# Stick-breaking attention with queries on partitions: sigmoids and a running product in place of softplus sums

## The chip, the cores and the metric

The kernel runs on one core of one Trainium2 chip. The metric is the device time of one execution in microseconds (us); lower is better.

## The reference, cut to what matters

One step of an encoder over 512 prompt rows (a new stream) and 32 sample rows (a running stream with 1024 cached keys). Layer 0 is a Mamba-2 layer, layer 1 a stick-breaking attention layer with 16 query heads of 64 on 4 key/value heads; each layer has two SwiGLU feed-forward parts (1024 to 2816), a gated embedding part and RMSNorms. All is float32. The part that the change touches:

```python
def sb_block(q, k, v, q0):
    # A[t,s] = sigmoid(z_ts) * prod_{s<j<t} (1 - sigmoid(z_tj)), keys s < t only
    z = jnp.einsum('bqhgd,bkhd->bhgqk', q, k) * (SB_HEAD_DIM ** -0.5)
    mask = jnp.arange(lk)[None, :] < q_pos[:, None]
    log_1m_beta = jnp.where(mask, jax.nn.log_sigmoid(-z), 0.0)
    log_a = z + lax.cumsum(log_1m_beta, axis=4, reverse=True)
    a = jnp.exp(jnp.where(mask, log_a, -jnp.inf))
    return jnp.einsum('bhgqk,bkhd->bqhgd', a, v)

q = h @ w_q;  o = sb_attention(q, k_all, v_all, q_start);  x = x + o @ w_o
```

The weight of a key is a sigmoid times the product of (1 - sigmoid) over all later keys; the reference forms it as exp(z - sum of softplus over this key and the later ones).

## The kernel before

Features lie on partitions and the 544 rows of both groups on columns. A dense product is split: weights and activations go into a high and a low float32 half (`whi`, `wlo`, `xh`, `xl`), and three products of 272 columns make one float32 product. Every instruction is recorded by one helper, so all of them have its line, L193, in the profile; groups are told apart by the names of what they write and read.

`attention(...)` is one stage near the end: query products (8 units of 1024x128 weights, each in two halves of 24 products), attention, output product (two units of 192 products of 272 columns each, one for each `a`). A key/value head is named by a pair (`a`, `b`) with both from 0 to 1; `e` (0 to 3) is the query head within it, `qb` a block of 128 queries, `kb` a block of 128 keys. `kT` holds the keys and `qT` the queries with features on partitions; `kk`, `kl` and `qq` are their halves, with high and low part of a head stacked on the 128 partitions, so that two products give one block of logits. Attention results are written back into `qT`, and `outputs` makes the halves `oh` and `ol` for the output product from it.

Keys lie on partitions. `block(kb, b)` makes the logits of one key block for all four heads of (`a`, `b`), 512 columns, in a PSUM bank `z`; the diagonal block gets the mask as a third product. `softplus` turns them into `zt` (or `run`) with ACT (Abs, Exp, Ln) and DVE; `halve` splits the result into `sh` and `sl`. The sum over later keys within the block is a product with the triangle `ntri`, that over all later key blocks one with a matrix of -1, `nones`, applied to the running sum `run`; both are added into the same bank `z`, two products each. ACT takes the Exp into `at`, and the value products of one key block (`o<-at,vt`, both `b` side by side) go into a bank `o`:

```python
def within():
    add(ps[:n], ntri[:n, :n], sh[:n])
    add(ps[:n], ntri[:n, :n], sl[:n], stop=True)
yield "T", 2 * t_cost(512) + 0.05, within
```

The sample rows run as one more stream of nine blocks (32 new keys, then eight blocks of 128 cached ones, `kc` and `vc`, each loaded by two transfers).

The order of all this comes from a planner, `Plan`. Each step is a generator that yields what it needs: `"get"` and `"put"` of a slot (PSUM banks `z`, `f`, `o`, and buffers), `"wait"` and `"set"` of events, and `("T" | "V" | "S" | "G", cost, emit)` for work on TensorE, VectorE, ScalarE and GpSimd (`"W"` is VectorE too; `either` and `pick` choose the less loaded engine). The planner takes the step that can start first by its costs, by rank where several can, and emits the instructions; the four engines keep that order. `NZ, NF1, NO = 5, 1, 2` gives the eight banks: five for logits, one for query products that are made between attention blocks, two for outputs. The first two units of query products use `z` banks and the later ones `f`. The first output product (`first_mix`) waits for the four blocks of `a` = 0 and the sample; its units then stand between the last blocks of `a` = 1.

Of the kernel before, what the change touches and what calls it, by code (L numbers as in the profile page):

```python
# [28 lines left out]
NZ, NF1, NO = 5, 1, 2  # L29

NSP, NZT, NAT, NRUN = 7, 4, 4, 4

RUNS = 2

BLOCKS = (1, 3, 2, 0), (3, 1, 2, 0)

MERGE, SB = 9, 7
# [3 lines left out]
RMIX, RHEAD = 0.15, 0.3  # L41
# [139 lines left out]
def _body(tc, io):  # L181
# [22 lines left out]
    with ExitStack() as ctx:  # L204
# [1274 lines left out]
        def attention(norm, after, ready, ahead, kT, vtok):  # L1479
            with ExitStack() as keep, \  # L1480
# [5 lines left out]
                def bank(tag, bufs=1):  # L1486
                    return pp.tile([P, 512], F32, tag=tag, name=tag, bufs=bufs)

                def two():
                    return [bank("z", NZ), bank("z", NZ)]  # L1490
# [23 lines left out]
                with tc.tile_pool(name="at", bufs=1, reuse_waits="tile") as tmp:  # L1514
                    ntri = tmp.tile([P, P], F32R, name="ntri")
                    tri = tmp.tile([P, 512], F32, tag="at", name="tri", bufs=NAT)[:, :P]
                    G.affine_select(out=tri, in_=ones, compare_op=ALU.is_ge, fill=0.0, base=0, pattern=[[-1, P]], channel_multiplier=1)
                    V.tensor_scalar(ntri, tri, -1.0, None, op0=ALU.mult)
                    mask = tmp.tile([P, P], BF16, name="mask")
                    G.memset(mask, 0.0)  # L1520
                    G.affine_select(out=mask, in_=mask, compare_op=ALU.is_gt, fill=BIG, base=0, pattern=[[1, P]], channel_multiplier=-1)
                    masks = mask[:TS, :TS].unsqueeze(1).to_broadcast([TS, 16, TS])
                    mask = mask[:, :].unsqueeze(1).to_broadcast([P, 4, P])
                    plan = Plan({"z": NZ, "f": NF1, "o": NO, "raw": 2, "s": NSP, "zt": NZT, "run": NRUN, "at": NAT, "cache": 3, "w": 2}, "a")
# [10 lines left out]
                    def key_parts(a):  # L1535
# [11 lines left out]
                        yield "set", ("keys", a)  # L1547
# [14 lines left out]
                    def softplus(t, z):  # L1562

                        if plan.load("S") <= plan.load("V"):
                            yield "S", s_cost(512, True), lambda: S.activation(t, z, AF.Abs)
                            yield "S", s_cost(512), lambda: S.activation(t, t, AF.Exp, scale=-1.0)
                            yield "S", s_cost(512), lambda: S.activation(t, t, AF.Ln, bias=1.0)
                            yield "W", v_cost(512), lambda: V.scalar_tensor_tensor(out=t, in0=z, scalar=0.0, in1=t, op0=ALU.max, op1=ALU.add)
                        else:
                            yield "W", v_cost(512), lambda: V.tensor_scalar(t, z, 40.0, None, op0=ALU.min)  # L1570
                            yield "S", s_cost(512), lambda: S.activation(t, t, AF.Exp)
                            yield "S", s_cost(512), lambda: S.activation(t, t, AF.Ln, bias=1.0)
                            yield "W", v_cost(512), lambda: V.tensor_tensor(out=t, in0=z, in1=t, op=ALU.max)

                    def halve(t, sh, sl):
                        yield copy(plan, 512, sh, t)
                        yield either(plan, v_cost(512), 1.225, lambda e: e.tensor_tensor(out=sl, in0=t, in1=sh.bitcast(F32), op=ALU.subtract))

                    def parts_tile():
                        return (tmp.tile([P, 512], F32R, tag="sh", name="sh", bufs=NSP),  # L1580
                                tmp.tile([P, 512], F32R, tag="sl", name="sl", bufs=NSP))

                    class Stream:


                        def __init__(self, name, last, halves):
# [297 lines left out]
                    with ExitStack() as keep2:  # L1884
# [10 lines left out]
                        for number, (st, kb) in enumerate(units):  # L1895
                            if st is sample:
                                number -= SB
# [271 lines left out]
```

## Time and profile before

| what | value |
| --- | --- |
| time, three runs | 2328.01, 2328.4, 2331.41 us; median 2328.4 |
| profiled execution | 2331.9 us, of it 2330.2 us span |
| attention stage (first query product to end of output product) | 1656.4 to 1880.2 us |
| DMA | 213 MB, mean 91 GB/s |

The span runs from the first to the last instruction that the profile shows. Busy time is what an engine's instructions are shown to last; matmuls are pipelined, so that one is shown longer than the distance to the next one's start. A row of the groups of instructions reads: engine, operation, output <- inputs, shape, count, then busy time in all and mean ns of one, then idle time just before them and who ended most of it. In a row of the timeline stand the start, the duration, the engine and the operation, and in brackets a wait and its releaser. A row of the windows gives for a stretch its length, then each engine's busy time with its number of instructions, then PEclk, the TensorE clock that was granted as a share of full speed, the DMA share and GB/s.

### The profile page before, as it was taken

How to read it: one execution, taken by the hardware profiler on the slowest of the kernel's cores; microseconds unless marked ns; L12 is line 12 of the kernel's file. 1: busy time of each engine (PE TensorE's matmuls, PEld its weight loads, DVE VectorE, ACT ScalarE, POOL GpSimd, SP SyncE). 2: the span in 40 equal slices, each digit the busy share in tenths (PEclk: the TensorE clock that was granted, in tenths of full speed). 3: DMA queues.
4: the chain of work that ended last, by engine and by line, in shares of the span. 5: the costliest groups of instructions: out<-in, count | busy, mean ns of one | idle time of the engine just before them, and what ended most of it. 6: DMA issues, size and time to landing. Idle time of an engine off the chain costs nothing.

```text
span 2330.2 us, 42548 instructions
## 1 busy us (share of the span) xinstructions
PE 2289.8 (98%) x17763; PEld 2214.1 (95%) x17763; DVE 1700.7 (73%) x2239; ACT 1045.1 (45%) x1531; POOL 584.7 (25%) x563
## 2 busy tenths in 40 slices
PE   9999999999999999999999999999998999999997
PEld 8999999989899999999999999999965799999997
DVE  7777786679677676777857677777688676777857
ACT  5333334557555453333345433333488553333343
POOL 1221222244324122212211122211243222222214
PEclk9999999999999999999999999999999999999999
DMA  5333323333333232233233333332211132333232
GB/s 161 89 91 106 95 73 91 107 97 99 111 92 89 82 117 84 90 109 91 73 101 98 112 100 92 91 109 63 85 49 32 37 118 78 105 97 99 65 104 75
DMA packets 112176, 213.17 MB, mean 91 GB/s; under 512 B 12528, under 2 KB 34672, under 8 KB 111984
## 3 DMA queue, kind: packets, MB, share of 16 engines
q1 hardware_dynamic: 109104, 204.92, 29.7%
q10 hardware_dynamic: 2880, 5.53, 0.7%
q8 instruction: 140, 2.29, 0.4%
q14 instruction: 52, 0.43, 0.1%
HBM read 204.83 MB, written 5.60 MB: 90 GB/s over the span
## 4 chain that ended last, share of the span: by engine, by line
PE 90%; DVE 4%; ACT 3%; issue 1%; POOL 1%; DMA 1%; SPq 0%; DVEq 0%; ACTq 0%; POOLq 0%
PE mm L193 81%; PE z L193 5%; PE aux L193 2%; PE o L193 1%; DVE wlo L193 1%; PE f L193 1%; ACT zt L193 1%; ACT whi L193 1%; POOL ab L193 1%; DVE xl L193 1%; DVE x L193 0%; DMA wraw<-in_wpg 0%; DVE fu L193 0%; ACT L193 0%; DVE rm L193 0%
## 5 line engine op out<-in xcount | busy, mean ns | idle before, releaser
L193 PE MATMUL mm<-xh,whi 128*128 128x272 f32 x2096 | 513.4, 293 | 2.2 <-ACT xh L193 1.2
L193 PE MATMUL mm<-xh,wlo 128*128 128x272 f32 x2096 | 507.1, 290 | 2.2 <-DVE wlo L193 2.2
L193 PE MATMUL mm<-xl,whi 128*128 128x272 f32 x2096 | 508.2, 290 | 0.3 <-DVE xl L193 0.3
L193 PEld LDWEIGHTS mm<-xh,whi 128*128 128x128 f32 x2096 | 359.6, 190 | 10.3 <-issue 7.4
L193 PEld LDWEIGHTS mm<-xh,wlo 128*128 128x128 f32 x2096 | 359.0, 190 | 2.9 <-DVE wlo L193 2.9
L193 PEld LDWEIGHTS mm<-xl,whi 128*128 128x128 f32 x2096 | 358.8, 190 | 0.5 <-DVE xl L193 0.5
L193 ACT ACTIVATE whi<-wraw 128x1024 fp32r<-128x1024 f32 (+3 forms) x217 | 186.6, 861 | 381.1 <-PE mm L193 261.3
L193 PE MATMUL mm<-xfh,whi 128*128 128x272 f32 x1152 | 332.0, 288 | 0.0
L193 PE MATMUL mm<-xfl,whi 128*128 128x272 f32 x1152 | 331.9, 288 | 0.0
L193 PE MATMUL mm<-xfh,wlo 128*128 128x272 f32 x1152 | 331.7, 288 | 0.0
L193 DVE TENSOR_TENSOR wlo<-wraw,whi 128x1024 fp32r<-128x1024 f32 (+3 forms) x252 | 256.1, 1017 | 72.9 <-ACT whi L193 53.6
L193 PE MATMUL mm<-hh,whi 128*128 128x272 f32 x1408 | 291.3, 288 | 0.0
L193 PE MATMUL mm<-hh,wlo 128*128 128x272 f32 x1408 | 290.8, 288 | 0.0
L193 PE MATMUL mm<-hl,whi 128*128 128x272 f32 x1408 | 290.7, 288 | 0.0
L193 ACT ACTIVATE whi<-a 128x1024 fp32r<-128x1024 f32 x127 | 135.0, 1063 | 321.3 <-PE mm L193 211.6
L193 DVE TENSOR_TENSOR wlo<-a,whi 128x1024 fp32r<-128x1024 f32 x145 | 178.4, 1230 | 103.5 <-ACT whi L193 69.0
L193 PEld LDWEIGHTS mm<-hl,whi 128*128 128x128 f32 x1408 | 221.2, 188 | 0.0
L193 PEld LDWEIGHTS mm<-hh,whi 128*128 128x128 f32 x1408 | 221.0, 188 | 0.0
L193 PEld LDWEIGHTS mm<-hh,wlo 128*128 128x128 f32 x1408 | 220.4, 188 | 0.0
L193 PEld LDWEIGHTS mm<-xfh,wlo 128*128 128x128 f32 x1152 | 216.8, 188 | 0.0
L193 PEld LDWEIGHTS mm<-xfl,whi 128*128 128x128 f32 x1152 | 216.7, 188 | 0.0
L193 PEld LDWEIGHTS mm<-xfh,whi 128*128 128x128 f32 x1152 | 216.7, 188 | 0.0
(293 smaller groups left out, 4195.3 us busy)
## 6 DMA issues: line engine op xcount, KB each, us to landing
a<-in_wgu SPq DMA_DIRECT2D x145, 512.0 KB, 4.0
wraw<-in_wd SPq DMA_DIRECT2D x128, 256.0 KB, 2.7
wraw<-in_win SPq DMA_DIRECT2D x41, 512.0 KB, 3.6
wraw<-in_wgu SPq DMA_DIRECT2D x29, 512.0 KB, 3.7
wraw<-in_wd SPq DMA_DIRECT2D x32, 384.0 KB, 3.1
ab<-acs_d SPq DMA_DIRECT2D x16, 512.0 KB, 4.7
wraw<-in_wout SPq DMA_DIRECT2D x16, 512.0 KB, 3.6
wraw<-in_wpg SPq DMA_DIRECT2D x16, 512.0 KB, 3.6
```

The costliest lines, as they stand in the source:

```text
L193: ins = getattr(self.engine, op)(*args, **kw)
```

## The change

Queries lie on partitions now, and keys along the columns. For a piece (`piece`: one `a`, `b`, `qb` and some heads `es`, together up to 512 columns) the logits of each head stand against all its keys, `(qb+1)*128` columns, with the query block as the stationary operand. ACT takes two sigmoids of the bank: `s` = sigmoid(z) into a buffer `p`, and sigmoid(-z) back into the bank. DVE runs a scan along the keys from the last to the first (`scan`), whose result `e` at a key is the product of sigmoid(-z) over it and all later ones; `p` times `e` shifted by one key is the weight. Since values are summed over keys, keys have to be on partitions again: TensorE transposes `p` in blocks of 128x128 into a bank `tr`, and ACT or DVE copies that into `at`. Value products then run per key block for the heads of a group. There are 44 pieces for the prompt.

The sample makes its 32 new keys at once and the 1024 cached ones in two halves of 512 for each (`a`, `b`), 8 pieces; a scan starts from the last result of the later half (`ends`). The cache comes in four loads of keys and four of values. The banks are divided 3 (`z`), 1 (`f`), 2 (`o`), 2 (`tr`). Buffers, ranks and the order of blocks change with it, the first query products use banks of all four kinds (`FIRSTQ`), ScalarE loads the table of sigmoids ahead of the stage in place of that with Exp and Ln, and `ntri`, `softplus`, `halve`, `run` and the products on them are gone.

```diff
-NZ, NF1, NO = 5, 1, 2
-NSP, NZT, NAT, NRUN = 7, 4, 4, 4
-BLOCKS = (1, 3, 2, 0), (3, 1, 2, 0)
+BANKS = {"z": 3, "f": 1, "o": 2, "tr": 2}
+NP, NE, NAT, NSA, NC = 6, 4, 8, 4, 3
+BLOCKS = (2, 3, 1, 0), (3, 2, 1, 0)
+HEADS = ([(0, 1, 2, 3)],), ([(0, 1), (2, 3)],), ([(0,), (1,)], [(2,), (3,)]), ([(0,), (1,)], [(2,), (3,)])
+FIRSTQ = ("z", "z"), ("z", "f"), ("o", "o"), ("tr", "tr")
...
-def softplus(t, z):
-    if plan.load("S") <= plan.load("V"):
-        yield "S", s_cost(512, True), lambda: S.activation(t, z, AF.Abs)
-        yield "S", s_cost(512), lambda: S.activation(t, t, AF.Exp, scale=-1.0)
-        yield "S", s_cost(512), lambda: S.activation(t, t, AF.Ln, bias=1.0)
-        yield "W", v_cost(512), lambda: V.scalar_tensor_tensor(out=t, in0=z, scalar=0.0, in1=t, op0=ALU.max, op1=ALU.add)
...
-def halve(t, sh, sl):
-    yield copy(plan, 512, sh, t)
-    yield either(plan, v_cost(512), 1.225, lambda e: e.tensor_tensor(out=sl, in0=t, in1=sh.bitcast(F32), op=ALU.subtract))
...
-at = self.at[kb, b] = tmp.tile([P, 512], F32, tag="at", name="at", bufs=NAT)
-yield "S", s_cost(512, True), lambda: S.activation(at[:n], ps[:n], AF.Exp)
...
+def gates(s, ps):
+    yield "S", cost, lambda: S.activation(s, ps, AF.Sigmoid)
+    yield "S", cost, lambda: S.activation(ps, ps, AF.Sigmoid, scale=-1.0)
+
+def scan(e, ps, first):
+    V.tensor_tensor_scan(e[:, ::-1], ps[:, ::-1], ones[:, :1].to_broadcast([P, e.shape[1]]), first, ALU.mult, ALU.mult)
+
+def piece(a, qb, b, es, at, first):
+    yield "get", "p"
+    yield "get", "z"
+    ps = bank("z")
+    def logits():
+        for i, e in enumerate(es):
+            z, q = ps[:, i * w:(i + 1) * w], qq[a, b][:, e, cols]
+            add(z, q, kk[a][b][:, :w], start=i == 0)
+            add(z, q, kl[a][b][:, :w])
+            add(z[:, qb * P:], identb, mask, stop=i == n - 1)
+    yield "T", n * (2 * t_cost(w) + 0.06) + 0.02, logits
+    yield from gates(s[:, :n * w], ps[:, :n * w])
+    yield "get", "e"
+    for i in range(n):
+        yield "W", 2 * w / 960.0 + 0.07, lambda: scan(t[:, part], ps[:, part], 1.0)
+    yield "put", "z"
+    yield either(plan, v_cost(n * w), 1.225, lambda e: e.tensor_tensor(out=sv[:, :, :w - 1], in0=sv[:, :, :w - 1], in1=tv[:, :, 1:], op=ALU.mult))
+    yield "put", "e"
+    yield "get", "tr"
+    yield "T", 0.11 * n * (qb + 1), lambda: transposed(...)
+    yield "put", "p"
+    yield out_of(n * w, at[...], tr[...])
+    yield "put", "tr"
+
+def mix(a, qb, heads, ats, first, n):
+    yield "wait", *[("at", a, qb, b, es) for b in range(2) for es in heads]
+    yield "get", "o"
+    for kb in range(qb, -1, -1):
+        yield "T", 0.23 * n + 0.02, emit
+    yield out_of(n * P, qT[a][...], out[...])
...
-    yield "S", 1.3, lambda: S.preload_act_table_set("natural_log_exp_and_others")
+    yield "S", 1.3, lambda: S.preload_act_table_set("sigmoid_and_others")
...
 def first_mix():
-    yield "wait", ("o", "s"), *[("o", (0, qb)) for qb in range(4)]
+    yield "wait", ("s", 0), *[("o", 0, qb, heads[0][0]) for qb in range(4) for heads in HEADS[qb]]
```

How the order changes is shown at three places. In the rows, the name ahead of the arrow is written and those behind it are read; the numbers tell instances apart. The first place is PE in the stretch in which no query products are left. Before:

```order
L193 MATMUL z_19830<-qq10_18783,kk10_18776 128x512
L193 MATMUL z_19830<-qq10_18783,kl10_18780 128x512
L193 MATMUL z_19768<-sh_19821,nones_93 128x512
L193 MATMUL z_19768<-sl_19822,nones_93 128x512
L193 MATMUL z_19768<-sh_19809,ntri_18765 128x512
L193 MATMUL z_19768<-sl_19810,ntri_18765 128x512
L193 MATMUL o_19795<-at_19867,vc_19637 64x128 x4
```

Logits of one block are followed by the sums of a block made earlier and by values of the sample. PE in the same stretch of the changed kernel (`identb` is the identity that carries the mask, `ident` that of the transposes):

```order
L193 MATMUL z_19789<-kk10_18774,qq10_18781 128x384
L193 MATMUL z_19789<-kl10_18778,qq10_18781 128x384
L193 LDWEIGHTS identb_282
L193 MATMUL z_19789<-mask_18765,identb_282 128x128
L193 MATMUL tr_19803<-ident_278,p_19740 128x128 x4
L193 MATMUL z_19804<-kk11_18775,qq11_19673 128x512
L193 MATMUL z_19804<-kl11_19676,qq11_19673 128x512
```

The transposes of an earlier piece stand where the sums stood, and every piece has its mask. The second place is DVE in the same stretch, where before the steps of softplus and of the running sum alternate:

```order
L193 SCALAR_TENSOR_TENSOR zt_19752<-z_19744,zt_19752 128x512
L193 COPY qT0_18760<-o_19274 128x4x128
L193 TENSOR_TENSOR run_19788<-run_19707,zt_19752 128x512
L193 TENSOR_TENSOR sl_19786<-zt_19752,sh_19785 128x512
L193 SCALAR_TENSOR_TENSOR zt_19777<-z_19768,zt_19777 128x512
L193 TENSOR_TENSOR run_19814<-run_19788,zt_19777 128x512
```

And in the changed kernel, where the scans (`e<-z,ones`) are printed under the name SCALAR_TENSOR_TENSOR:

```order
L193 SCALAR_TENSOR_TENSOR e_19840<-z_19804,ones_89 128x512
L193 SCALAR_TENSOR_TENSOR e_19852<-z_19825,ones_89 128x512
L193 SCALAR_TENSOR_TENSOR e_19856<-z_19789,ones_89 128x384
L193 SCALAR_TENSOR_TENSOR e_19891<-z_19857,ones_89 128x512
L193 TENSOR_TENSOR p_19800<-p_19800,e_19856 128x383
L193 SCALAR_TENSOR_TENSOR e_19902<-z_19871,ones_89 128x384
```

DVE runs mostly scans, one behind another, and some of the multiplications; the others are on POOL. The third place is PE at the output product (`z<-oh,whi` and its like). Before, the last sums and values of attention stand among its rows:

```order
L193 MATMUL z_20663<-ol0_20242,whi_20557 128x272
L193 MATMUL z_20663<-oh0_20241,wlo_20563 128x272
L193 MATMUL z_20338<-sh_20410,ntri_18765 128x512
L193 MATMUL z_20338<-sl_20411,ntri_18765 128x512
L193 MATMUL z_20358<-sh_20432,ntri_18765 128x512
L193 MATMUL z_20358<-sl_20433,ntri_18765 128x512
L193 MATMUL z_20395<-sh_20448,ntri_18765 128x512
L193 MATMUL z_20395<-sl_20449,ntri_18765 128x512
L193 MATMUL o_20260<-at_20478,vt0_14550 64x512
L193 MATMUL o_20260<-at_20680,vt0_14550 64x512
```

In the changed kernel the last transposes and values of attention come first:

```order
L193 MATMUL o_19981<-sa_20398,vc_20134 64x128
L193 MATMUL tr_20413<-ident_278,p_20339 128x128 x4
L193 MATMUL tr_20420<-ident_278,p_20355 128x128 x4
L193 MATMUL o_20430<-at_20075,vt0_14550 64x512
L193 MATMUL o_20430<-at_20076,vt0_14550 64x512
L193 MATMUL z_20438<-oh0_20219,whi_19583 128x272
L193 MATMUL z_20438<-ol0_20220,whi_19583 128x272
L193 MATMUL z_20438<-oh0_20219,wlo_19600 128x272
```

All 384 products of the output product now stand behind the last value product of attention, where part of the first 192 stood between its blocks.

More of the change, by code (lines that the diff above doesn't have):

```diff
@@ L1782, in dense @@
+                    def dense(feed, units, per, parts, done, tags=None):
                         n = len(parts)
@@ L1798, in dense @@
                                 for i in range(2):
[L1799 removed]
+                                    yield "spawn", leave(done, k, i, banks[i], tags[k][i])
                                 if k % per == per - 1:
```

400 lines of the change are left out of this document (175 added, 225 removed).

## The prediction

> **What bounds the kernel now.** I read the page first: its busy line and the chain that ended last.
>
> ```profile
> PE 2289.8 (98%) x17763; PEld 2214.1 (95%) x17763; DVE 1700.7 (73%) x2239; ACT 1045.1 (45%) x1531; POOL 584.7 (25%) x563
> PE 90%; DVE 4%; ACT 3%; issue 1%; POOL 1%; DMA 1%; SPq 0%; DVEq 0%; ACTq 0%; POOLq 0%
> ```
>
> PE carries nine tenths of the chain, so elsewhere only PE work counts. The change touches one stage; I took its first and last PE instruction from the timeline (first `z` matmul 1656.4, end of the output product 1880.2) and read the stage by windows cut at landmarks of PE's order: queries alone; query fill with first attention blocks; attention alone; first output product with the last blocks; second output product.
>
> ```profile
> core 0: us, PE busy (x) PEld busy (x) DVE busy (x) ACT busy (x) POOL busy (x), PEclk, DMA share, GB/s
> 1656.40:1686.50 30.10, 28.57 (x223) 28.03 (x222) 21.10 (x32) 15.41 (x20) 8.20 (x12) 1.00 0.24 79
> 1686.50:1736.50 50.00, 48.92 (x281) 36.84 (x280) 41.37 (x61) 38.36 (x67) 18.92 (x22) 1.00 0.15 43
> 1736.50:1818.40 81.90, 70.66 (x306) 40.87 (x305) 69.00 (x111) 72.68 (x138) 31.34 (x37) 0.94 0.11 32
> 1818.40:1855.40 37.00, 34.58 (x227) 29.80 (x225) 19.01 (x33) 11.91 (x21) 8.31 (x7) 0.95 0.18 47
> 1855.40:1880.20 24.80, 24.67 (x192) 24.24 (x192) 19.20 (x32) 12.55 (x22) 7.72 (x5) 1.00 0.25 73
> ```
>
> The stage is 223.8 us. In the third window PE, DVE and ACT are all 84 to 89% busy and none is full: they wait for each other in turn. There the change can win. PE's busy time hides its gaps, because one matmul is shown longer than the distance to the next, so I price PE by distance between starts:
>
> ```profile
> 1657.52 0.29 PE L193 MATMUL z<-xh,whi 128*128 128x272 f32 x1
> 1657.65 0.29 PE L193 MATMUL z<-xl,whi 128*128 128x272 f32 x1
> ...
> 1800.03 0.39 PE L193 MATMUL z<-sl,nones 128*128 128x512 f32 x1
> 1800.26 0.40 PE L193 MATMUL z<-sh,ntri 128*128 128x512 f32 x1
> ...
> 1803.23 1.08 PE L193 MATMUL o<-at,vt 128*64 128x512 f32 x4
> 1804.24 0.50 PE L193 MATMUL z<-qq,kk 128*128 128x512 f32 x1
> 1804.58 0.40 PE L193 MATMUL z<-qq,kl 128*128 128x512 f32 x1
> ...
> 454.26 0.66 PE L193 MATMUL aux<-ident,xs 128*128 128x128 f32 x4
> 454.75 0.27 PE L193 MATMUL aux<-ident,B 128*128 128x128 f32 x1
> ```
>
> So 0.125 us for a product of 272 columns, 0.233 for 512, 1.01 for the value products of one key block (both heads of a pair side by side), 0.12 for a float32 transpose of 128x128. The first product behind plain float32 takes 0.34 instead of 0.23 (1804.24), so each change of form costs about 0.1. Before's stage by these prices: 768 products of 272: 96.0; 80 logits, 162 sums and 17 masks at 0.233: 60.4; 20 value blocks: 20.2; sample logits, sample values and norm sums 14.6 (the same after, so their price doesn't matter); 59 changes of form 6. Together 197.2, so PE stands 26.6: 1.7, 1.3, about 18, 5 and 0.7 in the five windows.
>
> **PE: what goes and comes.**
>
> ```profile
> L193 PE MATMUL z<-sh,ntri 128*128 128x512 f32 x48 | 20.5, 427 | 0.0
> L193 PE MATMUL z<-sl,ntri 128*128 128x512 f32 x48 | 20.0, 417 | 2.3 <-DVE sl L193 2.3
> L193 PE MATMUL z<-sh,nones 128*128 128x512 f32 x32 | 14.8, 463 | 2.0 <-DVE zt L193 2.0
> L193 PE MATMUL z<-sl,nones 128*128 128x512 f32 x32 | 13.0, 405 | 0.0
> ```
>
> These 160 (and two narrow ones) go: 162 x 0.233 = -37.8. The 196 transposes come: x 0.12 = +23.5. Logits keep their columns but stand per head with 128 to 512 keys: 128 products and 64 masks, 27.5 instead of 22.6, +4.9. For 128 columns with a new 128x128 stationary no row of this type exists; bounds are 0.06 (a quarter of 512) and 0.12 (the transpose); I take 0.12 for products and 0.10 for masks, nearest in shape; the low end is 4 us less. Value products of two heads (256 columns) are paid at 0.58 instead of half of 1.01: 28 of them, +2.1. More changes of form, 78 for 59: +1.9. Sample logits and values keep their columns: 0. Sum -5.5: PE's work becomes about 191.7. Almost all of the removed PE time is spent again, so the gain has to come from the standing time.
>
> **DVE, ACT and POOL.**
>
> ```profile
> 1704.11 0.68 DVE L193 SCALAR_TENSOR_TENSOR zt<-z,zt 128x512 f32<-128x512 f32 x1
> 1704.70 0.68 DVE L193 TENSOR_TENSOR zt<-z,zt 128x512 f32<-128x512 f32 x1
> ...
> 433.05 0.48 DVE L193 TENSOR_TENSOR_SCAN acs<-keep,da 128x160 f32<-128x160 f32 x1
> 433.44 1.20 DVE L193 TENSOR_TENSOR wlo<-wraw,whi 128x1024 fp32r<-128x1024 f32 x1
> ```
>
> A 512-wide DVE operation takes 0.60 from start to start, the one scan of this kernel 0.39 for 160. If a scan has the same fixed part and twice the time per element, the two rows give 0.04 fixed and 2.19 ns per element, 1.16 for 512; scaled by length alone it is 1.25. I take 1.16; the other end adds 3 us to DVE in the third window.
>
> ```profile
> 1763.89 0.58 ACT L193 ACTIVATE run<-z 128x512 f32<-128x512 f32 x1
> 1764.37 0.62 ACT L193 ACTIVATE run<-run 128x512 f32<-128x512 f32 x1
> 1764.89 0.58 ACT L193 ACTIVATE at<-z 128x512 f32<-128x512 f32 x1
> ...
> 1772.71 1.28 POOL L193 TENSOR_TENSOR run<-run,zt 128x512 f32<-128x512 f32 x1
> ...
> L193 ACT ACTIVATE zt<-zt 128x512 f32<-128x512 f32 x51 | 31.2, 630 | 0.7 <-DVE zt L193 0.3
> ```
>
> ACT takes 0.48 per 512 out of PSUM and 0.52 out of SBUF; its third window (138 operations, of which the 51 steps inside softplus are the largest group) counted so is 68.5 of 81.9. Softplus, its split and the last exponential leave; two sigmoids per piece and most copies of transposes come. The second sigmoid is written back into PSUM, which no ACT row here does: between 0.48 (PSUM read) and 0.96 (if read and write of one bank take turns). I take 0.48, the row with the same source; the other end puts 15 us more on ACT, which makes it as full as PE and costs about 3. The Trainium skill, ScalarE: Activation LUTs, "Step-by-step: what each stage is for", calls PSUM the lower-latency destination for ScalarE; by it the sum would not rise, and no row here shows it.
>
> The third window after the change runs from the last query product to the last value product; its 33 pieces are 15,488 scan columns in 52 scans. Counts from the order: DVE 36 for scans (15,488 x 2.19 ns + 52 x 0.04), 8 for 22 multiplications (8 of them of one column), 11 for copies, key, query and output parts: 55. ACT 29.2 for sigmoids, 16.1 for copies, 4.6 for the rest: 50. POOL 19 multiplications at 1.0 to 1.4 by width and 7 others: 29 to 33. Behind a scan that waits for ACT's second sigmoid stand, on DVE, multiplications and the query results for which PE waits to get `f` back; behind a transpose that waits for its multiplication stand, on PE, the next logits; behind a copy that waits for its transposes, on ACT, the next sigmoids. None of these is free to pass. PE: logits 16.5 with the narrow price, transposes 15.1, values 14.2, sample 12.8, 39 changes of form 3.9: 62.5. The fullest engine falls from 68.5 (ACT) to 62.5 (PE), the second from 62.5 to 64 down to 55.
>
> **The sum.** First window 20.5 of PE work plus the same 1.7 = 22.2 (only the banks are taken in other order; the first logits need one head's query parts instead of four, and come 2.6 query halves earlier). Second: 231 query products 29.0, 16 pieces' and 4 more logits 11.1, 68 transposes 8.2, 28 value products in 14 pairs 8.1, 37 changes of form 3.7, together 60, plus 3 standing (one bank `f` between halves of 24 products, covered by pieces; before 1.3) = 63. Third: before, the fullest engine filled 68.5 / 81.9 = 0.84 of it; I keep that share, since chains and banks are as tight: 62.5 / 0.84 = 74.4. It includes the tail, in which the last pieces have no product left to cover them: before, the output product lay between (see the order). Last two: 48.2 plus 0.7 = 48.9. Together 208.5 against 223.8: -15.3. The profiled execution took 2331.9 us (span 2330.2 and 1.7 around it) and becomes 2316.6; the median shown is 2328.4, 3.5 lower, so 2313. Nothing after the stage changes. The sample's cache loads move the same bytes in half as many issues; the fourth pair waits for its slot, and the output weights behind it on SP are wanted only 12 us into the product; that cover is the DMA share of 0.11 in the third window. One table load replaces one.
>
> **Rivals.**
>
> *PE alone bounds the third window too.* The second window shows it: 48.7 of work in 50.0. For: every other engine has at least 12% less to do than PE. Against: three `z` banks instead of five, longer chains. 62.5 / 0.97 = 64.4, time 2303.
>
> *The standing stays.* The 26.6 are waits for hand-over, and a new hand-over (scan, transpose, copy) replaces each old one; then only PE's -5.5 is left: 2323. The change would have done nothing but its arithmetic.
>
> *The clock.* After a gap of 1.93 us the same product takes 0.23 instead of 0.13:
>
> ```profile
> 1824.78 0.39 PE L193 MATMUL z<-oh,whi 128*128 128x272 f32 x1 [1.93 <-ACT at L193]
> ...
> 1825.39 0.43 PE L193 MATMUL z<-oh,whi 128*128 128x272 f32 x1
> 1825.62 0.43 PE L193 MATMUL z<-ol,whi 128*128 128x272 f32 x1
> ```
>
> Granted clock was 0.94 in the third window. If short gaps around each transpose bring the mean to 0.82, 62.5 of work grows by 62.5 x (0.94 / 0.82 - 1) = 9: 2322. The Trainium skill, TensorE: Matmul & The Clock Gate, speaks for this: "A second HAM failure mode: psum-queue depth-cycling" says that micro-idles between groups cycling through PSUM banks make the gate swing, and "Part 4: PE-mode transpose" that transposes don't count as busy for it. The trace has the swing (0.94, the rows above); that transposes cause it no row shows, since those at 454 stand among long products.
>
> *Slower: the round trip of a `z` bank.* A bank is held from logits to the end of the scan. From the rows: 0.7 logits, 0.96 two sigmoids, 1.13 scan, about 0.4 of hand-overs (estimate), 3.2 alone; 4.8 with one foreign operation ahead on ACT and on DVE. Three banks and 33 pieces are 11 turns: at 6.8 a turn the banks fill 74.4, and from 8.1 on the gain is gone. At 8.5 the window is 93.5 and the time 2332; at 9, 2338. Against it: that takes 5 us of queueing per piece on engines that are 67% (ACT) and 74% (DVE) loaded.
>
> **How the numbers follow.** Forecast 0.5, own range 2307 to 2319. PE bound 0.2; clock 0.14; standing stays 0.09; banks 0.07. The range 2302 to 2324 reaches from the first rival to the clock and holds the dearer scan and sigmoid (+3 each) and the cheaper masks (-5). A measurement here tells 0.2%, 4.7 us: faster means under 2323.7. That is the forecast, the first rival and most of clock and standing: 0.86; the rest of those two and a part of the banks is no change: 0.08; slower 0.06.
>
> **What would show it.** Sums (`ntri`, `nones`) gone and 196 transposes at 0.12; a 512 scan shown with about 1.2; both sigmoids at 0.58; the last value product near 1656.4 + 160 = 1816, then 384 output products without a gap; the third window 74 long with PE gaps of 12 in all, most of them waits for DVE and ACT. Wrong would be: waits of logits for scans in most turns (banks), product distances of 0.23 over tens of us (clock), or a scan above 1.3.

## The result and the profile after

The changed kernel took 2304.1 us (median of 4, 2301.5 to 2308.2) against 2329.0 us: ratio 0.9893, 95% interval 0.9876 to 0.991. Measured once more beside the first experiments it was 2306.0 against 2327.8, ratio 0.9904 (0.9891 to 0.9918). It is faster by 22 to 25 us; 15.3 were forecast. The busy line and the chain of waits of the profiled execution (span 2299.8 us):

```profile
PE 2267.0 (99%) x17937; PEld 2207.0 (96%) x17937; DVE 1680.0 (73%) x2201; ACT 1011.1 (44%) x1489; POOL 575.7 (25%) x541
PE 92%; DVE 4%; ACT 2%; issue 1%; POOL 1%; DMA 1%; SPq 0%; DVEq 0%; ACTq 0%; POOLq 0%
```

Over the whole kernel PE lost 23 us of busy time, and its share of the chain rose. The stage by windows, cut at the first logits, the last query product and the first product of the output (the forecast's fourth and fifth window in one):

```profile
core 0: us, PE busy (x) PEld busy (x) DVE busy (x) ACT busy (x) POOL busy (x), PEclk, DMA share, GB/s
1649.65:1669.81 20.16, 20.16 (x159) 20.00 (x158) 15.62 (x23) 13.93 (x19) 4.15 (x7) 1.00 0.29 90
1669.81:1725.80 55.99, 55.97 (x427) 47.60 (x426) 42.86 (x56) 32.63 (x67) 22.88 (x22) 1.00 0.15 42
1725.80:1795.65 69.85, 62.82 (x431) 40.19 (x428) 60.64 (x101) 54.91 (x113) 25.65 (x24) 0.98 0.14 43
1795.65:1849.95 54.30, 51.05 (x385) 49.97 (x384) 30.41 (x53) 17.74 (x29) 11.15 (x7) 0.97 0.24 69
```

The stage is 200.3 us long instead of 223.8: -23.5, and that is the whole change. The spans of the two profiled executions differ by 30.4, but 6.8 of it lies ahead of the stage, in code that is the same; over all executions shown here the stage begins between 1649.7 and 1656.7 us. The length of the stage repeats far better (200.0 and 200.6 us in two executions of the changed kernel, first product to start of the last), so small effects are read from it below.

PE does not stand at all in the first two windows and 7.0 us in the third. In the fourth it stands 3.3 us, and some products behind those gaps run slower; together the window is 6.1 us longer than its 384 products at 0.1255 us, 48.2. Set against the rows of before, PE's busy time in the stage falls from 207.4 to 190.0 us and its idle time from 16.4 to 10.3: 17.4 and 6.1 of the 23.5 us. Busy time holds slowed products too, so this split is a rough one.

### The profile page after: what moved, and what is told of

The parts are those of the page before. It is cut to its first block, busy times and chain, and to the rows that moved or that the text cites. A ratio compares the mean times of both kernels' runs of the same rounds, so it can differ in the third digit from the quotient of the medians.

```text
span 2299.8 us, 42811 instructions
## 1 busy us (share of the span) xinstructions
PE 2267.0 (99%) x17937; PEld 2207.0 (96%) x17937; DVE 1680.0 (73%) x2201; ACT 1011.1 (44%) x1489; POOL 575.7 (25%) x541
## 4 chain that ended last, share of the span: by engine, by line
PE 92%; DVE 4%; ACT 2%; issue 1%; POOL 1%; DMA 1%; SPq 0%; DVEq 0%; ACTq 0%; POOLq 0%
PE mm L193 82%; PE z L193 3%; PE aux L193 3%; PE o L193 1%; PE f L193 1%; PE tr L193 1%; DVE wlo L193 1%; ACT whi L193 1%; DVE xl L193 1%; POOL ab L193 0%; DVE x L193 0%; DVE e L193 0%; DMA wraw<-in_wpg 0%; DVE fu L193 0%; DVE rm L193 0%
## 5 line engine op out<-in xcount | busy, mean ns | idle before, releaser
L193 PEld LDWEIGHTS mm<-xh,whi 128*128 128x128 f32 x2096 | 358.6, 189 | 10.5 <-issue 7.2
L193 DVE TENSOR_TENSOR wlo<-a,whi 128x1024 fp32r<-128x1024 f32 x145 | 178.4, 1230 | 101.7 <-ACT whi L193 67.2
```

The lines of the kernel that those rows point to most:

```text
L193: ins = getattr(self.engine, op)(*args, **kw)
```

## The experiments

All lengths are from the first query product to the start of the last output product, cut at the first logits, the last query product and the first output product. In the kernels built from the one before, and in the one with four z banks, some attention work falls into the last column. (The window rows of the changed kernel above are cut 0.16 us later at the last query product than the table.)

| kernel | queries | with pieces | attention alone | output | stage | time, ratio to before (95%) |
| --- | --- | --- | --- | --- | --- | --- |
| before | 30.1 | 50.0 | 88.3 | 55.1 | 223.5 | 2329.0 |
| changed | 20.2 | 55.8 | 70.0 | 54.0 | 200.0 | 2304.1, 0.9893 (0.9876 to 0.991) |
| changed, again | 20.2 | 55.8 | 70.5 | 54.1 | 200.6 | 2306.0, 0.9904 (0.9891 to 0.9918) |
| halves made early | 20.2 | 55.8 | 70.7 | 49.7 | 196.4 | 2302.3, 0.9892 (0.9878 to 0.9905) |
| transposes twice | 20.2 | 62.3 | 78.7 | 54.1 | 215.2 | 2321.7, 0.9972 (0.9962 to 0.9982) |
| no scan | 20.2 | 55.4 | 66.3 | 54.0 | 195.8 | 2302.9, 0.9896 (0.988 to 0.9913) |
| scan in SBUF | 20.2 | 62.4 | 77.7 | 54.0 | 214.2 | 2318.4, 0.9964 (0.9952 to 0.9976) |
| one sigmoid | 20.2 | 62.1 | 66.6 | 54.7 | 203.6 | 2309.8, 0.9929 (0.9914 to 0.9944) |
| early halves, four z banks | 20.2 | 59.1 | 67.2 | 52.6 | 199.0 | 2304.7, 0.9898 (0.9883 to 0.9912) |
| before, less PE | 30.1 | 47.4 | 86.6 | 55.0 | 219.1 | 2324.9, 0.9989 (0.998 to 0.9999) |
| before, less ACT | 30.1 | 52.1 | 83.0 | 54.7 | 219.9 | 2326.6, 0.9994 (0.9984 to 1.0004) |
| before, less ACT, order kept | 30.1 | 50.0 | 84.0 | 54.4 | 218.4 | 2323.8, 0.9978 (0.9968 to 0.9987) |
| before, blocks independent | 30.1 | 50.1 | 88.2 | 53.5 | 221.9 | 2327.8, 1.0003 (0.9993 to 1.0014) |
| before, less DVE | 30.1 | 49.5 | 88.8 | 53.5 | 222.0 | 2327.5, 0.9998 (0.9989 to 1.0007) |

**The changed kernel again.** No edit.

> The changed kernel once more, beside the experiments of the same chip: ratio to before 0.989 (2304 us), attention stage 200 us long, PE standing about 7 us between its 80th and 103rd us and about 3 us at the start of the second output product. If the gain of the first measurement hung on one execution, the ratio lies above 0.992.

The ratio held, the intervals overlap widely, and the stage is the same to 0.6 us.

**Where PE waits at the second output product.** In the changed kernel, ACT and then PE around the start of the output product for `a` = 1:

```profile
1795.76 0.60 ACT L193 ACTIVATE qT<-o 128x512 f32<-128x512 f32 x1 [0.53 <-PE o L193]
...
1819.98 1.06 ACT L193 ACTIVATE whi<-wraw 128x1024 fp32r<-128x1024 f32 x1 [5.01 <-PE z L193]
1820.94 2.65 ACT L193 ACTIVATE oh<-qT 128x272 fp32r<-128x272 f32 x8
```

```profile
1819.73 0.29 PE L193 MATMUL z<-oh,wlo 128*128 128x272 f32 x1
1821.41 0.52 PE L193 MATMUL z<-oh,whi 128*128 128x272 f32 x2 [1.39 <-ACT oh L193]
1822.70 0.39 PE L193 MATMUL z<-ol,whi 128*128 128x272 f32 x1 [0.78 <-DVE ol L193]
...
1823.96 0.43 PE L193 MATMUL z<-oh,whi 128*128 128x272 f32 x1
1824.19 0.43 PE L193 MATMUL z<-ol,whi 128*128 128x272 f32 x1
```

`qT` was complete at 1796.4, but the eight `oh` stand on ACT behind a weight split that waits 5 us for its slot. PE stands 1.4 and then 0.8 us, and the products behind the gap come at 0.23 instead of 0.125 for some three us. Before, the last sums and value products of attention lay over this hand-over. The edit makes the halves a step of the plan, ranked ahead of the weight splits, in free `at` tiles:

```diff
+def second_parts():
+    yield "wait", ("s", 1), *[("o", 1, qb, heads[0][0]) for qb in range(4) for heads in HEADS[qb]]
+    ...
+    for i in (1, 0):
+        for e, (h, l) in enumerate(second):
+            yield "spawn", second_part(h, l, e, slice(i * H, (i + 1) * H))
...
+plan.add(RM - 1.2, second_parts())
 plan.add(RM - 1, wo.fetch())
...
-parts = outputs(op, 1, ("oh", "ol"))
```

> Only the halves oh and ol of the second output product are made earlier: on ACT and DVE ahead of the last weight splits instead of behind them. Theory (the cover that the last attention blocks gave to that hand-over is gone, and PE waits there because in-order ACT has a weight split ahead of the halves): the gaps of 1.68 and 1.29 us and the 18 slow products behind them (0.1 us each) go, the stage falls from 200.3 to 195.5 to 196.5 and the time by 4 to 5 us. Rival (PE waits there for a free z bank or for the weights themselves): the same gap stays, 0 to 1 us.

```profile
1801.03 2.66 ACT L193 ACTIVATE oh<-qT 128x272 fp32r<-128x272 f32 x8
...
1800.43:1850.30 49.87, 48.73 (x385) 48.23 (x384) 30.16 (x53) 17.59 (x29) 11.15 (x7) 1.00 0.26 81
```

The halves are made at 1801, the gap is gone, the granted clock of the window is 1.00 instead of 0.97, and the stage is 4.2 us shorter than that of the changed kernel measured beside it. The theory holds. By time it is 2302.3 against 2306.0; the intervals of the two ratios overlap, and the first measurement of the changed kernel gave nearly the same ratio (0.9893 against 0.9892), so that it is the stage that shows it. This kernel has the lowest median time of the table.

**What a transpose costs, and whether PE has room.**

```diff
-for c in range(count):
-    TE.transpose(tr[:, c * P:(c + 1) * P], s(c), ident)
+for _ in range(2):
+    for c in range(count):
+        TE.transpose(tr[:, c * P:(c + 1) * P], s(c), ident)
```

> Every transpose is issued twice, 196 more, same result and same order. Theory (a transpose costs 0.09 us of PE and PE bounds the stage but for 7 us between its 80th and 103rd us): 17.6 more work, of it 2 to 6 swallowed by that standing, so the stage grows by 12 to 16 us. Rival 1 (0.12 each as priced in the prediction): 18 to 24 us. Rival 2 (hand-overs bound the attention-alone window, PE has room): 6 to 8 us, those of the window with query products alone.

```profile
1674.08:1736.36 62.28, 62.28 (x489) 54.53 (x488) 43.12 (x56) 33.35 (x66) 22.94 (x22) 1.00 0.13 39
1736.36:1815.02 78.66, 73.45 (x564) 53.02 (x562) 61.32 (x101) 56.09 (x113) 25.68 (x25) 1.00 0.12 38
```

The stage grew by 14.6 us. In the second window 68 more transposes cost 62.3 - 55.8 = 6.5, 0.095 each, with nothing to hide them. In the third, cut alike, PE's busy time rose by 10.5 for 128 (0.082 each), the window by 8.7, and the standing fell from 7.0 to 5.2. Work added to PE is paid in full in one window and to five sixths in the other. 0.12 each and "PE has room" are both out, and PE bounds the second window. That it bounds the third alone is not shown: four more transposes also make each piece's own chain some 0.36 us longer, and the run without scans, below, shortens that window while PE's instructions stay the same.

**The scan.** The replaced operation keeps operands and shape, and the order on all engines is the same.

```diff
-V.tensor_tensor_scan(e[:, ::-1], ps[:, ::-1], ones[:, :1].to_broadcast(...), first, ALU.mult, ALU.mult)
+V.tensor_tensor(out=e, in0=ps, in1=ones[:, :1].to_broadcast(...), op=ALU.mult)
```

> The changed kernel with each scan replaced by a plain multiplication of the same operands and shape (no running product; the weights are wrong), same order on all engines: a 512 wide one takes about 0.6 us instead of 1.2. Theory (PE bounds the stage but for the 5.7 us in which logits wait for scans): the stage falls by 4 to 6 us and the waits of logits for e are gone. Rival 1 (those waits are turns of the banks set by ACT's sigmoids as much as by the scan): 1 to 3 us. Rival 2 (DVE bounds more than the waits show): over 8 us.

What PE waited for in the third window, in the changed kernel and then without the scan (us in total, times, longest):

```profile
PE z L193 <- DVE e L193: 5.2, 6, 2.2
PE z L193 <- DVE en L193: 0.5, 1, 0.5
```

```profile
PE z L193 <- DVE e L193: 3.7, 4, 1.8
PE z L193 <- DVE en L193: 0.7, 1, 0.7
```

The third window without the scan, to be read beside the changed kernel's row above:

```profile
1726.43:1792.71 66.28, 60.65 (x431) 39.04 (x430) 46.80 (x100) 54.01 (x113) 25.57 (x24) 1.00 0.15 45
```

The stage fell by 4.2 us, as the theory said, but not for its reason: 13.8 us less for DVE in that window (46.8 for 60.6) took only 1.3 us off those waits. Most of the rest is PE's busy time, 60.65 for 62.82 with the same products, at a granted clock of 1.00 instead of 0.98. The theory's number was met and its mechanism mostly not: 4.4 us of waits of logits stayed with a scan half as long, so that the scan's length alone does not make them. That they are turns of the bank, of which the scan is only the last step, is the reading left, not a thing shown.

**A bank given back earlier.** The sigmoid of -z goes to the buffer `e` in SBUF, and the scan runs there in place. The edit also puts this sigmoid first and takes the buffer `e` ahead of both, so that each `e` is held longer.

```diff
+yield "S", cost, lambda: S.activation(t, ps, AF.Sigmoid, scale=-1.0)
 yield "S", cost, lambda: S.activation(s, ps, AF.Sigmoid)
-yield "S", cost, lambda: S.activation(ps, ps, AF.Sigmoid, scale=-1.0)
...
-yield from gates(s[:, :n * w], ps[:, :n * w])
 yield "get", "e"
...
+yield from gates(s[:, :n * w], ps[:, :n * w], t[:, :n * w])
+yield "put", "z"
...
-yield "W", 2 * w / 960.0 + 0.07, lambda: scan(t[:, part], ps[:, part], 1.0)
-yield "put", "z"
+yield "W", 2 * w / 960.0 + 0.07, lambda: scan(t[:, part], t[:, part], 1.0)
```

> The second sigmoid goes into the SBUF buffer e and the scan runs in place there, so that a z bank is given back after the two sigmoids and not after the scan. Theory (the 5.7 us that logits wait for scans are turns of three z banks): these waits go, the stage falls by 3 to 6 us. Rival (DVE and ACT together are what is full there, 84 and 83% busy in these 23.5 us): the waits move to the transposes, 0 to 1.5 us. A second rival (writing to SBUF costs ACT more than writing to PSUM): sigmoids longer than 0.59 us and the stage up by 1 to 3 us.

The stage is 14 us longer, a miss for all three. The waits of logits for scans did go, as the theory had it, and PE waits at the transposes instead, as the first rival had it, but far longer than its 1.5 us; the largest of these waits:

```profile
PE tr L193 <- POOL p L193: 7.3, 6, 1.8
```

Groups of the whole stage, two of the changed kernel and then the same two here:

```profile
L193 DVE TENSOR_TENSOR_SCAN e<-z,ones 128x512 f32<-128x512 f32 x16 | 19.3, 1213 | 4.6 <-ACT z L193 4.0 <-POOL p L193 0.7
L193 POOL TENSOR_TENSOR p<-p,e 128x511 f32<-128x511 f32 x16 | 19.2, 1202 | 22.3 <-DVE e L193 18.9 <-DVE p L193 3.3
```

```profile
L193 DVE TENSOR_TENSOR_SCAN e<-e,ones 128x512 f32<-128x512 f32 x20 | 29.4, 1478 | 1.7 <-ACT e L193 1.7
L193 POOL TENSOR_TENSOR p<-p,e 128x511 f32<-128x511 f32 x18 | 28.6, 1590 | 27.7 <-ACT at L193 9.9 <-DVE e L193 8.2 <-ACT e L193 3.1
```

A scan that reads SBUF takes 1.48 us on average instead of 1.21, and POOL's multiplication 1.59 instead of 1.20: the two hold each other up (the rows are in the last section). The bank in PSUM was not only a cost of this design; it also keeps DVE and POOL apart. Not all of the 14 us is shown to come from this: the planner also ordered the pieces anew, and ACT waits 7.4 us for `e` buffers, which are taken earlier here.

**ACT.** One sigmoid instead of two; the freed costs let the planner order the pieces anew.

```diff
-yield "S", cost, lambda: S.activation(s, ps, AF.Sigmoid)
 yield "S", cost, lambda: S.activation(ps, ps, AF.Sigmoid, scale=-1.0)
...
-out=sv[:, :, :w - 1], in0=sv[:, :, :w - 1], in1=tv[:, :, 1:], op=ALU.mult
+out=sv, in0=tv, in1=tv, op=ALU.mult
```

> The changed kernel with one sigmoid per piece instead of two (the multiplication takes the scan's result twice; the weights are wrong): 53 ACT operations of some 0.45 us go, 24 us. Theory (PE bounds all but the 7 us between its 80th and 103rd us of the stage): the stage falls by 2 to 5 us. Rival (ACT, 55 of 70 us busy in the attention-alone window and in every chain twice, sets its pace): 8 us or more.

```profile
1673.01:1735.14 62.13, 58.70 (x430) 49.48 (x429) 40.19 (x52) 25.52 (x49) 21.80 (x22) 0.95 0.15 46
1735.14:1801.78 66.64, 60.96 (x427) 40.50 (x425) 56.95 (x91) 41.13 (x80) 28.56 (x29) 0.97 0.13 38
```

With 24 us less work the stage is 3 us longer, a miss for both. The third window fell by 3.4 to 3.9 (against the two executions of the changed kernel) with 13.8 us less on ACT; the second, where PE had not stood at all, grew by 6: PE waits 3.4 us there, and its busy time is 2.9 longer at a granted clock of 0.95. As a measure of ACT's share the run is spoiled by the new order, and it says how much an order can be worth.

**Four z banks.** On top of the early halves (the norm of the queries then borrows `z` banks instead of `tr`):

```diff
-BANKS = {"z": 3, "f": 1, "o": 2, "tr": 2}
-FIRSTQ = ("z", "z"), ("z", "f"), ("o", "o"), ("tr", "tr")
+BANKS = {"z": 4, "f": 1, "o": 2, "tr": 1}
+FIRSTQ = ("z", "z"), ("f", "tr"), ("o", "o"), ("z", "z")
```

> The changed kernel with the halves of the second output product made early (worth 4.2 us in the earlier run) and with four z banks and one tr bank instead of three and two; the first query products take their banks in another order. Theory (the 5.7 us that logits wait for scans are turns of the z banks): those waits fall below 2 us and the stage falls by 3 to 5 us below that of the earlier run with the early halves (196.4), if one tr bank costs nothing. Rival (transposes then wait for the copy of the piece before, about 0.6 us each for ACT or DVE): new waits of transposes for at of 3 us and more, and the stage stays or grows by up to 6 us.

PE's waits in the second and third window:

```profile
PE z L193 <- DVE e L193: 3.1, 1, 3.1
PE tr L193 <- ACT at L193: 2.3, 5, 0.8
PE tr L193 <- DVE at L193: 1.7, 2, 1.0
```

With early halves alone the waits for scans were five, 5.1 us; the fourth bank leaves one of 3.1, and the single `tr` bank gives the gain back as waits of transposes for copies, 4.0 us here. The stage is 2.6 us longer than with early halves alone, as the rival said, with some attention work now behind the first output product. Of the two splits of the eight banks, three and two is the better by the stage; the two times (2304.7 and 2302.3) are not told apart by their ratios.

**Why PE stood in the attention-alone window of the kernel before.** The prediction put this at about 18 us by distances; the row below shows 13.2 us idle in 88.3. Four kinds of kernel take one thing away each. Less PE: the products of `sl` are left out.

```diff
-for part in self.sums[j, b]:
-    add(ps, nones, part)
+add(ps, nones, self.sums[j, b][0])
...
-add(ps[:n], ntri[:n, :n], sh[:n])
-add(ps[:n], ntri[:n, :n], sl[:n], stop=True)
+add(ps[:n], ntri[:n, :n], sh[:n], stop=True)
```

> The kernel before with the products of the low halves sl on ntri and nones left out (81 of 162, the low part of the sums is missing from the result); everything else, sl itself too, is kept. 81 x 0.233 = 18.9 us of PE's work go: 5.1 in the window with query products, 11.9 in the attention-alone window, 1.9 under the first output product. Theory (before, hand-overs between ACT, DVE and PE bound the attention-alone window, so PE's work alone is worth little there): the stage falls by 6 to 10 us. Rival (PE's arithmetic is what the change saved): 15 to 19 us.

Less ACT, once with the planner free and once with the order kept (the left-out steps stay in the plan and emit nothing; this is the edit shown):

```diff
-yield "S", s_cost(512), lambda: S.activation(t, t, AF.Exp, scale=-1.0)
-yield "S", s_cost(512), lambda: S.activation(t, t, AF.Ln, bias=1.0)
+yield "S", s_cost(512), lambda: None
+yield "S", s_cost(512), lambda: None
...
-yield "S", s_cost(512), lambda: S.activation(t, t, AF.Ln, bias=1.0)
+yield "S", s_cost(512), lambda: None
```

> The kernel before with the softplus cut short: where it was Abs, Exp, Ln and a maximum it is Abs and the maximum, and where it was a minimum, Exp, Ln and a maximum the Ln is left out; PE's work is unchanged (the weights are not those of the reference). About 25 us of ACT go in the attention-alone window. Theory (ACT's chain is the fullest there, 68.5 of 81.9 us): the window falls to about 72 to 75 and the stage by 7 to 11 us. Rival (PE's own work and the order of its products bound it): 0 to 3 us.

> The kernel before with the softplus cut short as in the earlier run (Exp and Ln left out behind Abs, Ln left out behind the other Exp; the weights are wrong), but now with the order of every engine kept word for word, so that only ACT has less to do: some 25 us in the attention-alone window. Theory (in-order ACT was what PE waited for there, 6.2 us for at and more through sh and sl): the stage falls by 8 to 12 us. Rival 1 (the chain of running sums from key block to key block): 0 to 3 us. Rival 2 (the hand-overs of many short steps, none of them alone): 3 to 6 us, and PE then waits for DVE or POOL instead.

No chain from key block to key block:

```diff
-for part in self.sums[j, b]:
-    add(ps, nones, part)
+for part in (sh, sl):
+    add(ps[:n], nones[:n, :n], part[:n])
```

> The kernel before with the products on nones taking the block's own halves sh and sl instead of those of the running sum over later key blocks (the weights are wrong): the same instructions in the same order with the same work, but no key block waits for the one behind it any more. Rival 1 (that chain paced the attention-alone window, and the scan does away with it): 6 to 12 us less. Theory (it did not; the waits of the nones products are 2 us and those for sl 2.3): 1 to 4 us less.

Less DVE:

```diff
-V.scalar_tensor_tensor(out=t, in0=z, scalar=0.0, in1=t, op0=ALU.max, op1=ALU.add)
+V.scalar_tensor_tensor(out=t[:, :64], in0=z[:, :64], scalar=0.0, in1=t[:, :64], op0=ALU.max, op1=ALU.add)
...
-V.tensor_tensor(out=t, in0=z, in1=t, op=ALU.max)
+V.tensor_tensor(out=t[:, :64], in0=z[:, :64], in1=t[:, :64], op=ALU.max)
```

> The kernel before with the last DVE step of each softplus on 64 of its 512 columns (the weights are wrong), same instructions, same order on all engines: 49 steps of 0.6 us shrink to about 0.15, some 20 us less for DVE, about 13 of them in the attention-alone window. Theory (PE, DVE and ACT fill that window together and wait for each other in turn, so that relief of one is worth little): the stage falls by 2 to 6 us, as with PE alone (4.4) and ACT alone (5.1). Rival (DVE was the engine that set the pace there, which would explain why PE and ACT alone brought little): 9 us or more.

The stretch from the last query product to the first output product, one row for each kernel: before, less PE, less ACT (order kept), blocks independent, less DVE.

```profile
1736.50:1824.80 88.30, 75.13 (x330) 44.12 (x328) 74.50 (x120) 77.94 (x148) 35.27 (x41) 0.94 0.10 30
1732.40:1818.98 86.58, 66.62 (x275) 35.18 (x273) 74.98 (x119) 77.28 (x148) 35.70 (x41) 0.92 0.11 31
1734.13:1818.10 83.97, 75.02 (x329) 43.75 (x328) 74.50 (x118) 50.09 (x90) 36.04 (x41) 0.94 0.11 32
1734.36:1822.55 88.19, 75.52 (x329) 44.15 (x327) 74.79 (x120) 77.95 (x148) 35.18 (x41) 0.94 0.10 30
1733.83:1822.61 88.78, 76.24 (x330) 43.99 (x328) 62.37 (x120) 77.37 (x148) 34.76 (x41) 0.92 0.10 30
```

PE has 8.5 us less to do and the stretch falls by 1.7; ACT 27.9 less, 4.3; DVE 12.1 less, nothing; no chain, nothing. With the stage as a whole, less PE brought 4.4 of the 18.9 us reckoned, under the 6 to 10 that the theory gave; less ACT 5.1, under its 8 to 12 and in the second rival's range, and 3.6 with the planner free, between that theory (7 to 11) and its rival; the other two 1.6 and 1.5, at or under the low end of the theory, and that under the output product, not in this stretch. By time these last two cannot be told from before (1.0003 and 0.9998). None of the four set the pace alone. PE, DVE and ACT were busy for 84 to 88% of the stretch. That they wait for each other in turn, so that whichever is relieved two others are left, fits all the rows; no run relieves two of them at once. In two rows, less PE and less DVE, the granted clock was also 0.92 instead of 0.94.

## Why the prediction was right, and where it was wrong

The direction and the range held. The reason for the gain held only in part: of the 15.3 us the prediction gave 5.5 to PE's work and the rest to its standing time, and PE's work fell about three times as far (an estimate, worked out below). The likeliest case's own range, 2307 to 2319, missed by 1 to 3 us: the stage was forecast at 208.5 and is 200.3. By windows, work and standing of PE (measured: busy time and the rest; in the last row the 384 products at 0.1255 and the rest):

| window | forecast | measured |
| --- | --- | --- |
| queries | 20.5 + 1.7 | 20.2 + 0 |
| with pieces | 60 + 3 | 56.0 + 0 |
| attention alone | 62.5 + 11.9 | 62.8 + 7.0 |
| output | 48.2 + 0.7 | 48.2 + 6.1 |

*The price of transposes and of changes of form* failed in the second window, where work alone counts. From the changed kernel's timeline:

```profile
1700.97 0.23 PE L193 MATMUL z<-mask,identb 128*128 128x128 bf16 x1
1701.04 0.61 PE L193 MATMUL tr<-ident,p 128*128 128x128 f32 x4
1701.40 0.38 PE L193 MATMUL f<-xh,whi 128*128 128x272 f32 x1
1701.61 0.29 PE L193 MATMUL f<-xl,whi 128*128 128x272 f32 x1
...
1705.01 1.52 PE L193 MATMUL o<-at,vt 128*64 128x256 f32 x12
1706.46 0.40 PE L193 MATMUL f<-xh,whi 128*128 128x272 f32 x1
```

Four transposes take 0.36, the mask ahead of them 0.03 more than elsewhere, and the product behind them 0.21 instead of 0.125: 0.47 in all. The prediction paid 4 x 0.12 and 0.1 for the change of form, 0.58. Its 0.12 came from one group of four at 454.26, which took 0.49 to the next row; another group in the same execution takes 0.43:

```profile
439.46 0.60 PE L193 MATMUL aux<-ident,xs 128*128 128x128 f32 x4
439.89 0.27 PE L193 MATMUL aux<-ident,B 128*128 128x128 f32 x1
```

So one long row was charged to all 196 transposes, and a change of form on top. Value products of three key blocks of 256 columns take 1.45, 0.48 each, about the half of 1.01; 0.58 is what a single block alone takes (1709.65 to 1710.24), and it was charged to all. From a mask to the next product it is 0.04 to 0.07, not 0.10.

*"Almost all of the removed PE time is spent again"* failed with these prices. The third window has the same transposes, values and masks, so its 62.5 was too dear as well, which the table hides: there busy time stands for work, and the prediction had set busy time aside because it hides gaps. With 0.09 for its 128 transposes, 0.48 for its 14 pairs of value products and 0.04 to 0.07 for its 40 masks, its work comes to about 56 us (an estimate), and what PE loses to standing and slowed products to about 14, near the 11.9 forecast. The stage's work is then 20.2 + 56.0 + 56 + 48.2, about 180, and not 191.7: 17 us less than the 197.2 of before, and 6 to 7 us less standing, as the profile's own busy and idle time have it (17.4 and 6.1).

*The standing of the second window* (3) and of the first (1.7) did not come: one bank `f` was covered.

*The fullest engine's share, 0.84,* held better than its 62.5 did: 56 of 69.85 is 0.80. By the profile's busy time, for like with like, it was 77.94 / 88.30 = 0.88 before (ACT) and is 62.82 / 69.85 = 0.90 now (PE). So the window became shorter about as its fullest engine's load did, 15 us of busy time for 18 of the window. Before, three engines had nearly the same load (75, 74, 78 us in one stretch), and the experiments show that relief of one of them is worth little; the change takes from all three, and most from ACT, whose third window is 54.9 us (50 forecast) beside 62.8 for PE. DVE has 60.6 (55 forecast). That relief of all at once is what shortens the window is what is left after the single ones; that it alone does is not shown, since hand-over, planner's order and loads change together in the real kernel.

*"Last two windows: 48.2 plus 0.7"* failed the other way. The prediction said that the output product no longer lies between the last pieces, and priced the tail of attention for it, where PE then stood half a us only; the loss was 24 us later, where the second output product had lost its cover. The early halves gave 4.2 of the 5.4 us back.

Two errors of opposite sign thus hid each other in part: 13.6 us too much in the first three windows, 5.4 too little in the last. That the total came so near is to this extent luck.

*The rivals.* "PE alone bounds the third window too" forecast 2303 and met the time, but not by its mechanism: that window is 69.85, not 64.4, and PE bounds the second instead more tightly than it said. "The standing stays" is out. "The round trip of a z bank" is real but small: three banks cost about 5 us of waits, at pieces with scans of 384 and 512 columns, between 1729.4 and 1752.9 us:

```profile
1729.40:1752.90 23.50, 17.82 (x98) 10.85 (x97) 19.72 (x32) 19.42 (x42) 12.02 (x11) 0.93 0.22 66
```

"The clock" is out for transposes: twice as many of them ran at a granted clock of 1.00 in both windows. It falls to 0.93 in the row above, where PE stands for 5.7 of 23.5 us; the 0.82 of that rival stands in no row of these windows. The Trainium skill, TensorE: Matmul & The Clock Gate, in "Part 4: PE-mode transpose", says that transposes do not count as busy for the gate; here, between other products, no row shows a loss from it.

*What it said would show it:* no `ntri` or `nones` left, transposes at 0.09 instead of 0.12, a 512 scan at 1.21 and both sigmoids at 0.597 us (1.2 and 0.58 forecast), the last value product 146 us into the stage instead of 160, gaps of 7 instead of 12 us, and then gaps in the output product that it had excluded. The group of the sigmoids written back into PSUM, whose price had been open between 0.48 and 0.96, and that of those written to SBUF:

```profile
L193 ACT ACTIVATE z<-z 128x512 f32<-128x512 f32 x36 | 21.2, 597 | 0.0
L193 ACT ACTIVATE p<-z 128x512 f32<-128x512 f32 x36 | 21.2, 597 | 9.8 <-PE z L193 9.2
```

They cost the same.

## What to carry to other kernels

Where three engines are each 85% busy and none is full, ask how much the change takes from all of them (what these runs suggest and do not prove): here 8.5, 12 or 28 us of PE, DVE or ACT alone bought 1.7, 0 and 4.3, while the change took 12, 14 and 23 us from PE, DVE and ACT together and the stretch lost 18. When work that was interleaved is moved away, list every hand-over that it lay over, also those far behind it. Compare shares only in one measure: busy time with busy time, distances with distances. Price an operation with its change of form once, from a whole group of rows up to the first product that runs at its usual distance again, and keep the planner's order fixed in experiments that leave work out, or the order is what is measured.

## What the runs showed of the hardware

The scan in SBUF was the surprise. Reading PSUM, it and POOL's multiplication run side by side without loss (changed kernel, DVE, then POOL):

```profile
1697.57 1.21 DVE L193 TENSOR_TENSOR_SCAN e<-z,ones 128x512 f32<-128x512 f32 x1
```

```profile
1697.28 1.09 POOL L193 TENSOR_TENSOR p<-p,e 128x511 f32<-128x511 f32 x1 [1.72 <-DVE e L193]
```

With the scan reading SBUF the means are 1.48 and 1.59 us, and the rows show how they come about. The 512-wide scans that have no multiplication on POOL beside them still take 1.19 to 1.28. Those that overlap with one take up to 2.11. In the two pairs below, the one that starts first keeps its usual time and the other is stretched: first the scan ahead, then POOL ahead (DVE, then POOL in each pair):

```profile
1745.35 1.19 DVE L193 TENSOR_TENSOR_SCAN e<-e,ones 128x512 f32<-128x512 f32 x1
1745.55 1.88 POOL L193 TENSOR_TENSOR p<-p,e 128x511 f32<-128x511 f32 x1 [1.51 <-DVE e L193]
```

```profile
1747.63 2.04 DVE L193 TENSOR_TENSOR_SCAN e<-e,ones 128x512 f32<-128x512 f32 x1
1747.39 1.20 POOL L193 TENSOR_TENSOR p<-p,e 128x511 f32<-128x511 f32 x1
```

The Trainium skill, SBUF — State Buffer, "Who interferes with whom", has the rule: a DVE instruction with two inputs in SBUF contends with a GpSimd instruction that reads SBUF, and one with at most one does not, outside the modes that use two ports. The rows agree: the scan's other input, `ones`, is in SBUF, so that moving the first one there made it two.
